# A gated decoder step: partial sums of the second projection added on chip, and the first chunk's loads moved from POOL's queue to ACT's

## The chip, the cores and the metric

The kernel runs on one core of one Trainium2 chip. The metric is device time in microseconds (us), from the start of the program to its end. A core has five engines with queues of their own: PE (TensorE, matrix products into the PSUM banks; PEld is its weight load), DVE (VectorE), ACT (ScalarE), POOL (GpSimd) and SP (SyncE, here only a DMA queue). SP, ACT and POOL issue DMAs, and an instruction that waits holds up everything behind it on its engine.

## The reference

One layer of a hybrid decoder over 1024 prompt tokens and 8 sample tokens (1032 columns in the kernel), D_MODEL 2048. Two branches, a retention and a diagonal state space model, are projected back to 2048 columns, gated, summed and projected once more:

```python
proj = h @ w_in
q, k, v, za, ub, zb, ga, gb = jnp.split(proj, splits, axis=-1)
ya, s_ret_new = retention(q, k, v, pos, s_ret)
ya = (ya * jax.nn.silu(za.astype(F32))).astype(x.dtype) @ w_pa
yb, s_re_new, s_im_new = s5(ub, ...)          # ends in a GLU: y * sigmoid(y @ w_glu + b_glu)
yb = (yb * jax.nn.silu(zb.astype(F32))).astype(x.dtype) @ w_pb
merged = jax.nn.sigmoid(ga) * ya + jax.nn.sigmoid(gb) * yb
out = merged @ w_out
return x + rmsnorm(out, g_post), s_ret_new, s_re_new, s_im_new
```

All is float32. The change concerns `merged` (the sum of the two gated projections) and the start of `merged @ w_out`.

## The kernel before, in words

Each float32 operand is split into two float32r halves, `hi` (a cast on ACT) and `lo` (the remainder, a subtraction on DVE), and a product is three matmuls: hi*hi, hi*lo, lo*hi. Every operand of PE thus costs one ACT cast and one DVE subtraction, for weights (`whi`, `wlo`) and tokens (`a`, function `split`).

The stages on PE in order: the input projection `w_in` in two halves of the contraction; the GLU (`w_glu`, lines 1475 and 1476); the gated projections `w_pa` (8 pairs of row tiles) and `w_pb` (8 pairs, p = 0 to 7); and `w_out`, first the last 392 tokens (`out_rows`, 16 outputs of 4 weight quarters each), then the first 640 (`out_tokens`).

The projections use a scheme of seven products per 2 x 2 block: for each pair of row tiles (2p, 2p+1) and two column halves of HT = 516 tokens, products n = 0 to 6, each 24 matmuls. `evac_p` takes a product out of PSUM, and the blocks "11", "22", "21", "12" are complete at n = 2, 4, 5, 6. The column half c is 1 for "22" and "12".

`gated` then multiplies a block by its gate `zz` (loaded on ACT's queue by `load_z` two products ahead). In `w_pa` the block is stored to `pap_d`. In `w_pb` POOL issues a DMA that adds the `pap_d` block onto the tile in place (`accum_op`), and LAG = 4 products later a second DMA that stores the merged tile to `mg_d`. Only the last pair's c = 1 blocks load `pap_d` to chip and add on DVE or POOL.

For `w_out` each of 16 merged row tiles m is split again. Tokens 640 to 1031 are needed first: tiles 0 to 11 are loaded back (`mg_load`, tile `mga`, on ACT's queue), tiles 12 to 15 are taken from the tiles still on chip (`last_t`; tiles 12 and 13 belong to pair 6, 14 and 15 to pair 7). Tokens 0 to 639 are loaded and split by `fill` while `out_rows` runs, through two slots of one large tile `z`.

The order on each engine is that of the code, with work put behind product g by `at(g, ...)` and run by `late_work(g)`; background generators in `bg` advance one `yield` per `slot()`, that is per product or per weight quarter. `left_over` runs what the last gate of `w_in` (sigmoids `u<-u`, `p<-p` on ACT after an accumulating DMA) still has due when the GLU starts.

Of the kernel before, what the change touches and what calls it, by code (L numbers as in the profile page):

```python
# [10 lines left out]
F32 = mybir.dt.float32  # L11
# [16 lines left out]
TA = 640  # L28
SW = TOK - TA
THIRDS = [(0, 384), (384, 768), (768, TOK), (TA, TOK)]  # L30
HT = TOK // 2
# [47 lines left out]
def emit(ctx, tc, I, O):  # L79
    nc = tc.nc  # L80
    V, A, P, T = nc.vector, nc.scalar, nc.gpsimd, nc.tensor

    def tt(out, a, b, op, eng=None):
        return (eng or V).tensor_tensor(out, a, b, op)  # L84

    def mul(out, a, b, eng=None):
        tt(out, a, b, ALU.mult, eng)

    def add(out, a, b, eng=None):
        return tt(out, a, b, ALU.add, eng)  # L90
# [34 lines left out]
    def dram(name, shape):  # L125
        return dr.tile(shape, F32, name=name)
# [18 lines left out]
    mg_d = dram("mg_d", [16, 128, TOK])  # L145
# [34 lines left out]
    def drain():  # L180
        while bg:
            slot()
# [617 lines left out]
    def popen(name, side, bufs):  # L800
        st = ExitStack()
        return st, st.enter_context(tc.tile_pool(name=name, bufs=bufs, side=side))
# [9 lines left out]
    NP = len(pairs)  # L812
    steps = [(kh, p) for kh in range(2) for p in range(NP)] + [(kh, p) for kh in ("pa", "pb") for p in range(8)]
# [83 lines left out]
    def two(t):  # L897
        return t.rearrange("p (j c) -> p j c", j=2)
# [9 lines left out]
    def at(g, f):  # L908
        due.setdefault(g, []).append(f)
# [324 lines left out]
    def late_work(g):  # L1234
        with ExitStack() as after:
            for ins in anchor.values():
                after.enter_context(tc.issue_after(ins))
            for f in due.pop(g, ()):
                f()
# [4 lines left out]
    for s in range(2 * NP):  # L1244
        kh, p = steps[s]
# [40 lines left out]
        for n in range(7):  # L1286
            g = 7 * s + n
# [28 lines left out]
    gstack.close()  # L1316

    def left_over():
        for n in range(2, 8):
            yield  # L1320
            for g in sorted(due):
                if g - 14 * NP <= n - (n > 4) - 2:
                    late_work(g)


# [5 lines left out]
    zz_tile = lambda: zzp.tile([128, HT], F32, name="zz")  # L1331
    opened = {}

    def fx_open():
        opened["fx"], opened["fxp"] = popen("fx", "left", 4)
# [145 lines left out]
    zq = {}  # L1481
    AT = {"11": (0, 0), "22": (1, 1), "21": (1, 0), "12": (0, 1)}
    last_t = {}

    def load_z(s, name):
        kind, p = steps[s]
        r, c = AT[name]
        zq[name] = zz_tile()
        A.dma_start(zq[name], (sga_d if kind == "pa" else sgb_d)[2 * p + r, :, HT * c:HT * c + HT])
        if s == len(steps) - 1 and c:  # L1490
            zq[name, "p"] = zz_tile()
            A.dma_start(zq[name, "p"], pap_d[2 * p + r, :, HT * c:HT * c + HT])

    def gated(g, name, t, ps=None):
        s = g // 7
        kind, p = steps[s]
        r, c = AT[name]
        m, cols = 2 * p + r, slice(HT * c, HT * c + HT)
        z = zq.pop(name)
        if ps is None:  # L1500
            mul(t, t, z)
        else:
            mul(two(t), ps, two(z))
        if kind == "pa":
            P.dma_start(pap_d[m, :, cols], t)
        elif (name, "p") in zq:
            add(t, t, zq.pop((name, "p")), P if name == "22" else V)
            last_t[m] = t
            P.dma_start(mg_d[m, :, HT:TA], t[:, 0:TA - HT])
        else:  # L1510
            P.dma_start(t, pap_d[m, :, cols], accum_op=ALU.add)
            at(g + LAG, lambda: P.dma_start(mg_d[m, :, cols], t))  # L1512
            if s == len(steps) - 2 and c:
                last_t[m] = t

    def evac_p(g, ps):
        n = g % 7
# [39 lines left out]
    SE = len(steps) - 1  # L1557
    mg_order = deque(range(2, 12))
    nxt = done_q = 0
    for s in range(S0, len(steps)):  # L1560
        kind, p = steps[s]
        if s == S0 + 1:
            opened["stg"].close()
            fx_open()
            bg.append(make_forms(yb_d, fb_d))
        if s == S0 + 6:
            drain()
            stg_open(8)
        if s == S0 + 9:
            opened["stg"].close()  # L1570
            mgstack, mgp = popen("mgp", "left", 6)
        for n in range(7):
            g = 7 * s + n
            if n == 1:
                fetch(s + 1)
            prep(g + 2)
            evac_p(g, product(g))
            if n in (0, 2, 3, 4):
                at(g, lambda s=s, n=n: load_z(s, {0: "11", 2: "22", 3: "21", 4: "12"}[n]))
            if s == S0 and n < 6:  # L1580
                for _ in range((2, 1, 1, 1, 2, 1)[n]):
                    at(g, lambda o=order_q[pa_q[0]]: unstage("pa", *o))
                    if pa_q[0] + 8 < 28:
                        at(g, lambda o=order_q[pa_q[0] + 8]: stage(opened["stgp"], "pa", *o))
                    pa_q[0] += 1
            q = g - 7 * (S0 + 6)
            if 0 <= q < 4:
                for _ in range(2):
                    at(g, lambda o=order_q[nxt]: stage(opened["stgp"], "pb", *o))
                    nxt += 1  # L1590
            if 3 <= q < 20:
                for i in range(1 if q < 7 else 2):
                    if done_q < 28:
                        at(g, lambda o=order_q[done_q]: unstage("pb", *o))
                        done_q += 1
                        if nxt < 28:
                            at(g, lambda o=order_q[nxt]: stage(opened["stgp"], "pb", *o))
                            nxt += 1
            if s == SE - 1 and n in (1, 2, 3):
                for m in (2 * n - 2, 2 * n - 1):  # L1600
                    at(g, lambda m=m: mg_load(m))
            if s == SE - 1 and n in (5, 6):
                at(g, lambda m=n - 5: mg_split(m))
            if s == SE and n < 6:
                for m in (2 + 2 * n, 3 + 2 * n):
                    at(g, lambda m=m: mg_split(m, last_t[m][:, TA - HT:HT] if m in last_t else None))
                for m in (6 + 2 * n, 7 + 2 * n) if n < 3 else ():
                    at(g, lambda m=m: mg_load(m))
            late_work(g)
            slot()  # L1610
    for m in (15, 14):
        mg_split(m, last_t[m][:, TA - HT:HT])
    for g in sorted(due):
        late_work(g)
    mgstack.close()
    zstack.close()
    estack.close()
# [18 lines left out]
    def out_rows():  # L1636
        t0, w, per = TA, TOK - TA, 5
        ssq = stl.tile([128, SW], F32, name="sp")[:, 0:w]
        rb = rstd[:, 0:w]
        zt, slots = {}, {}  # L1640
        slots[3] = free.pop()
        zt[3] = flat(slots[3])

        def fill():

            place = lambda m: zt[3][:, w + TA * (m % 2):w + TA * (m % 2) + TA]

            def ld(m):
                P.dma_start(place(m), mg_d[m, :, 0:TA])

            ld(0)
            ld(1)
            for m in range(KD):
                for _ in range(2):
                    yield
                split((mg[m][0][:, 0:TA], mg[m][1][:, 0:TA]), place(m))
                yield
                if m + 2 < KD:
                    ld(m + 2)

        bg.append(fill())

        def z_of(m):
            return zt[m // per][:, (m % per) * w:(m % per + 1) * w]

        def evac_out(m):
            def f(_, ps):
                if m < 15 and m % per == 0:
                    slots[m // per] = free.popleft()
                    zt[m // per] = flat(slots[m // per])  # L1670
                if m == 0:
                    A.activation(ssq, ps, AF.Square)
                else:
                    s = st_tile()[:, 0:w]
                    A.activation(s, ps, AF.Square)
                    add(ssq, ssq, s, P)
                A.activation(z_of(m), ps, AF.Copy, scale=gpost[:, m:m + 1])
            return f

        def finish():  # L1680
            yield
            yield
            yield from rms_bcast(ssq, rb, stl)
            for m in range(16):
                z = z_of(m)
                x = stl.tile([128, SW], F32, name="sz")[:, 0:w]
                nc.sync.dma_start(x, I["xT"][m, :, t0:TOK])
                yield
                mul(z, z, rb)
                add(z, z, x)  # L1690
                P.dma_start(O["yA"][m], z)
                if m % per == per - 1 or m == 15:
                    free.append(slots[m // per])
                yield

        for m in range(16):
            linear(I["w_out"], m, KD, lambda k: mg[k], evac_out(m), thirds=(3,))
        bg.append(finish())
# [182 lines left out]
```

## Time and profile before

| | us |
|---|---|
| median of 3 runs | 2634.81 (2631.14 to 2636.29) |
| the profiled execution, its own time | 2632.4 |
| its span in the trace | 2630.6 |
| PE busy | 2596.9 |
| the GLU's first and last matmul | 1822.1 and 1914.5 |
| last matmul of `w_pb` starts | 2237.5 |
| first matmul of `w_out` | 2246.1 |

The rows shown further down come from one profiled execution. A row of the timeline has the start, the duration, the engine, the line, the operation, the tile written and the tiles read, a count, and in brackets how long the engine stood idle before it and for what. A row of the waits reads "who <- for whom: total us, times, longest". A row of the windows has its bounds and length, then the busy time and instructions of each engine, the granted PE clock (1.00 is full), the busy share of the 16 DMA engines and GB/s. `u`, `p` and `st` are the tiles of a block, `pp` its partial sum after the change, `acc` and `mm` PSUM banks.

### The profile page before, as it was taken

The page shows a single profiled execution, that of the slowest core. Times are in us where ns is not written, and L with a number is a line of the kernel's source. Part 1 is how long each engine was busy: PE and PEld are TensorE (multiplying, and loading weights), DVE is VectorE, ACT ScalarE, POOL GpSimd, SP SyncE. Part 2 cuts the span into 40 slices and gives each one's busy share as a digit, 9 for nine tenths or more (in the row PEclk, how much of TensorE's full clock was granted, in tenths as well). Part 3 has the DMA queues.
Part 4 walks back from the last instruction along what each step waited for, and adds up shares of the span by engine and source line. Part 5 has one row for each costly group of instructions (what it writes and reads, how often), then busy time and mean ns, then how long its engine had stood idle before and what let it go on. Part 6 is the DMA issues. An engine that isn't in the chain of part 4 may idle for free. (4 is left out here: it accounts for less than half of the span.)

```text
span 2630.6 us, 51277 instructions
## 1 busy us (share of the span) xinstructions
PE 2596.9 (99%) x19652; PEld 2532.8 (96%) x19652; DVE 1840.2 (70%) x3852; ACT 956.6 (36%) x1679; POOL 716.5 (27%) x1173
## 2 busy tenths in 40 slices
PE   9999999999999999999999999999999999899998
PEld 8999999999999999999999999999999999798886
DVE  6655989889889867558876656666477866444555
ACT  6113233333323325443234544444332423343343
POOL 0103322222222222332244433333422322211011
PEclk9999999999999999999999999999999999899999
DMA  5896444444444457886689787869777788655666
GB/s 191 260 269 208 151 122 125 132 126 122 126 127 123 130 162 216 208 216 165 153 212 252 204 208 201 214 168 278 244 240 239 241 196 229 195 157 176 190 200 229
DMA packets 228789, 499.85 MB, mean 190 GB/s; under 512 B 32432, under 2 KB 54912, under 8 KB 228416
## 3 DMA queue, kind: packets, MB, share of 16 engines
q0 software_dynamic: 94704, 274.47, 38.2%
q1 hardware_dynamic: 103072, 179.57, 22.5%
q10 hardware_dynamic: 30768, 42.54, 5.4%
q8 instruction: 154, 2.52, 0.4%
q14 instruction: 91, 0.75, 0.1%
HBM read 340.57 MB, written 155.89 MB: 189 GB/s over the span
## 5 line engine op out<-in xcount | busy, mean ns | idle before, releaser
L892 PE MATMUL acc<-a,whi 128*128 128x258 f32 x9632 | 1562.3, 284 | 1.0 <-ACT whi L873 0.6
L892 PEld LDWEIGHTS acc<-a,whi 128*128 128x128 f32 x9632 | 1326.6, 190 | 5.4 <-issue 2.4
L892 PE MATMUL acc<-a,wlo 128*128 128x258 f32 x4816 | 969.1, 282 | 0.0
L892 PEld LDWEIGHTS acc<-a,wlo 128*128 128x128 f32 x4816 | 744.7, 189 | 0.0
L84 DVE TENSOR_TENSOR wlo<-wraw,whi 128x512 fp32r<-128x512 f32 x482 | 331.2, 687 | 242.9 <-ACT whi L202 139.9
L873 ACT CAST whi<-wraw 128x512 fp32r<-128x512 f32 x344 | 213.8, 622 | 618.5 <-PE acc L892 508.0
L873 ACT CAST whi<-wr 128x512 fp32r<-128x512 f32 x258 | 160.3, 621 | 515.6 <-PE acc L892 442.0
L209 PE MATMUL mm<-a,whi 128*128 128x384 f32 (+2 forms) x704 | 235.0, 335 | 17.6 <-ACT whi L202 9.4
L210 PE MATMUL mm<-a,whi 128*128 128x384 f32 (+2 forms) x704 | 234.4, 333 | 0.2 <-DVE a L363 0.2
L211 PE MATMUL mm<-a,wlo 128*128 128x384 f32 (+2 forms) x704 | 233.4, 332 | 0.1
L84 DVE TENSOR_TENSOR wlo<-wr,whi 128x512 fp32r<-128x512 f32 x273 | 187.2, 686 | 50.4 <-ACT whi L873 29.8
L1779 PE MATMUL mm<-whi,a 128*128 128x512 f32 x512 | 171.1, 395 | 0.0
L202 ACT CAST whi<-wraw 128x512 fp32r<-128x512 f32 x138 | 85.5, 621 | 205.0 <-PE mm L210 95.3
L209 PEld LDWEIGHTS mm<-a,whi 128*128 128x128 f32 x704 | 133.8, 190 | 18.7 <-ACT whi L202 9.9
L211 PEld LDWEIGHTS mm<-a,wlo 128*128 128x128 f32 x704 | 134.5, 191 | 1.7 <-DVE wlo L84 1.6
L210 PEld LDWEIGHTS mm<-a,whi 128*128 128x128 f32 x704 | 134.1, 190 | 1.0 <-DVE a L363 0.9
L84 DVE TENSOR_TENSOR wraw<-wr 128x512 f32<-128x512 f32 x172 | 118.2, 687 | 7.0 <-DMA wr<-in_w_pa 4.7
L1779 PEld LDWEIGHTS mm<-whi,a 128*128 128x128 f32 x512 | 96.2, 188 | 22.8
L84 DVE TENSOR_TENSOR p<-acc,p 128x516 f32<-128x516 f32 x86 | 59.6, 693 | 81.7 <-PE acc L892 81.5
L84 DVE TENSOR_TENSOR u<-acc,u 128x516 f32<-128x516 f32 x86 | 59.7, 694 | 63.1 <-PE acc L892 61.8
L84 DVE TENSOR_TENSOR u<-acc,p 128x516 f32<-128x516 f32 x86 | 59.6, 693 | 62.5 <-PE acc L892 62.1
L1779 PE MATMUL mm<-wlo,a 128*128 128x512 f32 x256 | 101.3, 396 | 0.0
(368 smaller groups left out, 3423.4 us busy)
## 6 DMA issues: line engine op xcount, KB each, us to landing
wr<-in_w_in SPq DMA_DIRECT2D x280, 256.0 KB
pt_d<-u POOLq DMA_DIRECT2D x70, 258.0 KB, 3.3
u<-pt_d POOLq DMA_DIRECT2D x70, 258.0 KB, 5.2
wraw<-in_w_outB SPq DMA_DIRECT2D x66, 256.0 KB
stg<-fm_d POOLq DMA_DIRECT2D x44, 258.0 KB, 4.4
wx<-in_w_outB SPq DMA_DIRECT2D x43, 256.0 KB
wraw<-in_w_out SPq DMA_DIRECT2D x39, 256.0 KB
pt_d<-st POOLq DMA_DIRECT2D x35, 258.0 KB, 3.1
```

The costliest lines, as they stand in the source:

```text
L84: return (eng or V).tensor_tensor(out, a, b, op)
L202: anchor["a"] = A.copy(hi, raw).ins
L209: T.matmul(ps, wh[:, i, :], xh[:, t0:t1], start=first, stop=False)
L210: T.matmul(ps, wh[:, i, :], xl[:, t0:t1], start=False, stop=False)
L211: anchor["p"] = T.matmul(ps, wl[:, i, :], xh[:, t0:t1], start=False, stop=last).ins
L873: anchor["a"] = A.copy(hi, f).ins
L892: anchor["p"] = T.matmul(ps[:, j, 0:258], a[:, i, :], b[:, 258 * j:258 * j + 258], start=first and i == 0 and a is wh and b is xh, stop=n ...
L1779: anchor["p"] = T.matmul(ps[c], a, b, start=k == 0 and a is xh and b is wh, stop=k == KD - 1 and a is xl).ins
```

## The change

- `load_z` loads the partial sum `pap_d` into a new pool `pp` of four tiles for every block from pair 2 on, on ACT's queue, right behind the block's gate.
- `gated` adds it on DVE (on POOL for three blocks of the last pair) and stores the merged tile at once, all its columns. Pairs 0 and 1 keep the accumulating DMA. `mga` has five tiles in place of six, and its first loads are spread over the pair before the last.
- `fill` issues its loads on ACT's queue, a slot later than before, and gives the first one six slots before its split in place of two.
- `left_over` runs the last gate's three sigmoid steps at slots 4, 6 and 9. On ACT the last of them then stands behind the first three GLU evacuations (L1423) and not ahead of them, and three casts of the forms for `w_pa` (`a<-fx`), not two, stand ahead of the first.

```diff
     def left_over():
-        for n in range(2, 8):
+        for n in range(12):
             yield
             for g in sorted(due):
-                if g - 14 * NP <= n - (n > 4) - 2:
+                if n >= {1: 4, 2: 6, 3: 9}[g - 14 * NP]:
                     late_work(g)
...
-        if s == len(steps) - 1 and c:
-            zq[name, "p"] = zz_tile()
+        if kind == "pb" and p > 1:
+            zq[name, "p"] = ppp.tile([128, HT], F32, name="pp")
             A.dma_start(zq[name, "p"], pap_d[2 * p + r, :, HT * c:HT * c + HT])
...
         elif (name, "p") in zq:
-            add(t, t, zq.pop((name, "p")), P if name == "22" else V)
-            last_t[m] = t
-            P.dma_start(mg_d[m, :, HT:TA], t[:, 0:TA - HT])
+            add(t, t, zq.pop((name, "p")), P if p == 7 and name != "12" else V)
+            if c and p > 5:
+                last_t[m] = t
+            P.dma_start(mg_d[m, :, cols], t)
         else:
             P.dma_start(t, pap_d[m, :, cols], accum_op=ALU.add)
             at(g + LAG, lambda: P.dma_start(mg_d[m, :, cols], t))
-            if s == len(steps) - 2 and c:
-                last_t[m] = t
...
-            mgstack, mgp = popen("mgp", "left", 6)
+            mgstack, mgp = popen("mgp", "left", 5)
+            ppstack, ppp = popen("pp", "left", 4)
...
-            if s == SE - 1 and n in (1, 2, 3):
-                for m in (2 * n - 2, 2 * n - 1):
+            if s == SE - 1 and n in (1, 2, 5, 6):
+                for m in (2 * n - 2, 2 * n - 1) if n < 3 else (n - 1,):
                     at(g, lambda m=m: mg_load(m))
...
             def ld(m):
-                P.dma_start(place(m), mg_d[m, :, 0:TA])
-
+                A.dma_start(place(m), mg_d[m, :, 0:TA])
+
+            yield
             ld(0)
             ld(1)
             for m in range(KD):
-                for _ in range(2):
+                for _ in range(2 if m else 6):
                     yield
```

How the built program moves, at three places. POOL, from the last pair's first block on, before (`z` is the large tile of the output stage, `sp` and `st` at the end are sums of squares there):

```order
L1511 DMA st<-pap_d 128x516
L1512 DMA mg_d<-st 128x516
L84 TENSOR_TENSOR u_27954<-u_27954,zz 128x516
L1509 DMA mg_d<-u_27954 128x124
L1511 DMA p_27822<-pap_d 128x516
L1512 DMA mg_d<-p_27822 128x516
L1509 DMA mg_d<-u_27867 128x124
L1632 DMA z_28106<-in_g_post_row 128x2048
L1649 DMA z_28110<-mg_d 128x640 x5
```

The same stretch of POOL after the change:

```order
L84 TENSOR_TENSOR st<-st,pp 128x516
L1510 DMA mg_d<-st 128x516
L84 TENSOR_TENSOR u_28001<-u_28001,pp 128x516
L1510 DMA mg_d<-u_28001 128x516
L84 TENSOR_TENSOR p_27868<-p_27868,pp 128x516
L1510 DMA mg_d<-p_27868 128x516
L1510 DMA mg_d<-u_27915 128x516
L1633 DMA z_28154<-in_g_post_row 128x2048
L84 TENSOR_TENSOR sp<-sp,st 128x392 x15
```

The accumulating DMAs (L1511) and the loads of the 640-token chunk (L1649) have left this queue.

DVE around the last PSUM evacuation, which is `u_27867<-acc` before (`a<-u` are the second halves of the splits of tiles 12 to 15, `wlo` those of weights):

```order
L84 TENSOR_TENSOR u_27954<-u_27954,zz 128x516
L84 TENSOR_TENSOR a_28037<-u_27602,a_28037 128x392
L84 TENSOR_TENSOR wlo<-wraw,whi 128x512
L84 TENSOR_TENSOR p_27822<-acc,p_27822 128x516
L84 TENSOR_TENSOR a_28040<-u_27675,a_28040 128x392
L84 TENSOR_TENSOR p_27822<-p_27822,zz 128x516
L84 TENSOR_TENSOR wlo<-wraw,whi 128x512
L84 TENSOR_TENSOR u_27867<-acc,u_27867 128x516
```

After the change it is `u_27915<-acc`:

```order
L84 TENSOR_TENSOR p_27868<-acc,p_27868 128x516
L84 TENSOR_TENSOR a_28086<-u_27642,a_28086 128x392
L84 TENSOR_TENSOR p_27868<-p_27868,zz 128x516
L84 TENSOR_TENSOR a_28089<-u_27716,a_28089 128x392
L84 TENSOR_TENSOR wlo<-wraw,whi 128x512
L84 TENSOR_TENSOR u_27915<-acc,u_27915 128x516
L84 TENSOR_TENSOR a_28120<-u_28001,a_28120 128x392
L84 TENSOR_TENSOR u_27915<-u_27915,zz 128x516
L84 TENSOR_TENSOR wlo<-wraw,whi 128x512
L84 TENSOR_TENSOR u_27915<-u_27915,pp 128x516
```

The two splits of pair 6's tiles now stand behind the evacuation of n = 5, and a sum `u<-u,pp` follows the last gate.

ACT from the last weight casts of the gated stage into `w_out`, before (`whi` are casts of weight quarters, `a<-z` of the 640-token chunk):

```order
L256 CAST a_28075<-u_27867 128x392
L202 CAST whi<-wx_28105 128x512
L202 CAST whi<-wraw 128x512 x2
L1672 ACTIVATE sp<-mm 128x392
L1677 ACTIVATE z_28192<-mm,gpost 128x392
L202 CAST whi<-wraw 128x512
L256 CAST a_27751<-z_28110 128x640
```

And after:

```order
L256 CAST a_28123<-u_27915 128x392
L202 CAST whi<-wx_28153 128x512
L1650 DMA z_28158<-mg_d 128x640 x2
L202 CAST whi<-wraw 128x512 x2
L1674 ACTIVATE sp<-mm 128x392
L1679 ACTIVATE z_28238<-mm,gpost 128x392
L202 CAST whi<-wraw 128x512
L202 CAST whi<-wx_28152 128x512
L256 CAST a_27795<-z_28158 128x640
```

The first two loads stand between the fifth and the sixth weight cast of `w_out`, and in the built program they wait for the stores of the six last merged tiles but the `st` ones, since `z` lies over those buffers. In the built program each DMA of SP or ACT also waits for the DMA that used its completion semaphore last, of eight that the two queues take in turn: a pair had eight such DMAs (four weights, four gates) and now has twelve.

More of the change, by code (lines that the diff above doesn't have):

```diff
@@ L1614, in emit @@
         late_work(g)
+    ppstack.close()
     mgstack.close()
```

## The prediction

> **What bounds the kernel now.** I read the page's busy shares and clock row first, then the list of waits of TensorE (PE), then PE's own rows around each wait, and from there the engine that each wait names.
>
> ```profile
> PE 2596.9 (99%) x19652; PEld 2532.8 (96%) x19652; DVE 1840.2 (70%) x3852; ACT 956.6 (36%) x1679; POOL 716.5 (27%) x1173
> PEclk9999999999999999999999999999999999899999
> ...
> PE mm L209 <- ACT whi L202: 9.4, 2, 5.2
> PE mm L209 <- DVE u L84: 8.2, 1, 8.2
> PE acc L209 <- ACT p L1423: 1.3, 1, 1.3
> ...
> PE acc L209 <- ACT u L1423: 0.4, 1, 0.4
> ```
>
> PE is the bound: 99% busy, and the clock row has one slice under full. So a change pays only where PE stands still or runs slowly. Of the waits (total, times, longest), 5.2 us of the first line is the load at the kernel's start. What stays is 8.2 and 4.2 us, both at the seam between the last gated product and the output projection, and 1.3 + 0.4 us early in the GLU. The windows of the seam:
>
> ```profile
> core 0: us, PE busy (x) PEld busy (x) DVE busy (x) ACT busy (x) POOL busy (x), PEclk, DMA share, GB/s
> ...
> 2206.00:2238.00 32.00, 31.91 (x264) 31.52 (x263) 21.62 (x36) 12.08 (x23) 8.96 (x12) 1.00 0.93 255
> 2238.00:2246.10 8.10, 0.00 (x0) 0.01 (x1) 4.19 (x8) 2.06 (x4) 2.07 (x3) 0.68 0.71 164
> 2246.10:2251.20 5.10, 5.08 (x16) 5.10 (x17) 1.36 (x3) 0.83 (x2) 2.43 (x4) 0.50 0.67 223
> 2251.20:2265.90 14.70, 14.69 (x82) 14.35 (x80) 4.82 (x8) 4.09 (x8) 3.62 (x6) 1.00 0.75 218
> 2265.90:2270.10 4.20, 0.04 (x1) 0.04 (x1) 1.40 (x2) 2.06 (x4) 0.54 (x1) 0.78 0.37 127
> 2270.10:2275.10 5.00, 5.00 (x15) 4.56 (x16) 2.99 (x6) 3.17 (x6) 2.06 (x3) 0.50 0.80 238
> ```
>
> After each hole the granted clock is 0.50 for about 5 us: 16 and 15 matmuls, where the full-clock window does 82 in 14.70, that is 0.179 us each. Each hole therefore costs its idle time and a slow restart. Why the first hole lasts:
>
> ```profile
> 2226.43 0.70 DVE L84 TENSOR_TENSOR st<-acc,zz 128x516 f32<-128x516 f32 x1
> 2242.13 0.93 POOL L1511 DMA_DIRECT2D st<-pap_d  x1
> POOL mg_d L1512 <- DMA u<-pap_d: 47.1, 14, 6.8
> ...
> 2241.36 0.52 ACT L256 CAST a<-u 128x392 fp32r<-128x392 f32 x1 [6.71 <-DMA u<-pap_d]
> 2241.91 0.57 DVE L84 TENSOR_TENSOR a<-u,a 128x392 fp32r<-128x392 f32 x1 [6.04 <-ACT a L256]
> 2245.28 0.69 DVE L84 TENSOR_TENSOR u<-acc,u 128x516 f32<-128x516 f32 x1
> 2246.12 0.67 PE L209 MATMUL mm<-a,whi 128*128 128x392 f32 x1 [8.21 <-DVE u L84]
> ```
>
> POOL issues the accumulating DMA and behind it, in order, the store that must wait for it. It is 15.0 us late by the last pair (2226.43 + 0.70 to 2242.13). So the sum of row tile 12 arrives late, ACT's cast of it waits 6.71 us, DVE's half of that split waits for ACT, and the last PSUM evacuation (u<-acc,u) stands behind it on DVE; PE can't have the banks before. The second hole hangs on the same queue: POOL gets to the first loads of the 640-token chunk only at 2260.92, ACT blocks on one, and the weight casts queue behind.
>
> ```profile
> 2260.92 1.16 POOL L1649 DMA_DIRECT2D z<-mg_d  x2
> 2266.82 0.72 ACT L256 CAST a<-z 128x640 fp32r<-128x640 f32 x1 [5.81 <-DMA z<-mg_d]
> 2270.06 0.69 PE L209 MATMUL mm<-a,whi 128*128 128x392 f32 x1 [4.17 <-ACT whi L202]
> ```
>
> **The change, part by part.**
>
> *First hole.* From pair 2 on, 22 accumulating DMAs leave POOL (of 30; two sums of the last pair were made on chip already), and no store there waits for a DMA any more. The casts of tiles 12 and 13 need only a DVE add of the pair before. In the new order DVE meets, after evacuation n=5 (PE ends at 2246.12 - 8.21 = 2237.91; at 264 matmuls in 31.91 us its product of 24 takes 2.9, so n=5 is ready at 2235.0): a cast's remainder, the gate, a second remainder and one weight remainder, then the last evacuation: with n=5 itself five operations ahead of it of 0.56 to 0.70 us, which brings the start of the last one to about 2238.0, 0.1 us after PE's end. From the start of that evacuation to PE's start the rows above show 0.84 us (2245.28 to 2246.12). So 0.95 us of the 8.21 remain: gain 7.3. The upper end is 7.4 (no lateness). For the lower end there is one row of doubt, the loads of tiles 10 and 11 that stand ahead:
>
> ```profile
> ACT a L256 <- DMA mga<-mg_d: 2.7, 2, 2.0
> ```
>
> If that wait, now hidden, came a second time, 3.7 us would remain and the gain be 4.5. I take 7.3: these loads are issued at the same product as before, with POOL's backlog gone.
>
> *Clock after it.* 5.10 - 16 x 0.179 = 2.2 us. A pause of 0.95 us is nearer to the one of 1.34 us in the GLU than to the 4.17:
>
> ```profile
> 1833.40:1834.90 1.50, 0.16 (x3) 0.01 (x1) 1.02 (x2) 1.45 (x3) 1.07 (x2) 1.00 0.99 402
> 1834.90:1840.00 5.10, 4.67 (x25) 4.35 (x26) 5.07 (x10) 3.14 (x6) 2.05 (x4) 1.00 0.75 240
> ```
>
> There the clock stayed at 1.00. So the 2.2 us go (0 if the pause stays long).
>
> *Second hole.* The loads move to ACT, issued about one weight quarter into the first output row, and the first split waits six quarters in place of two. But the first load has to wait for the last store of a merged tile, whose buffer lies under it. That store follows, on DVE, the last evacuation, a remainder, the gate, a weight remainder and the new add (0.6 us a step from 2238.0): issued at 2241.4.
>
> ```profile
> DMA to landing us min/median/max: 1.9/3.6/7.2
> L1551 ACTq DMA_DIRECT2D mga<-mg_d x12: 326/378/499, 2200.8 to 2226.9; - x12
> ```
>
> The first row is of all DMAs on the merged tensor. With the median the store lands at 2245.0 and ACT, having issued both loads (2 x 0.4), casts the sixth quarter by 2246.4. PE, started at 2238.9, needs it four quarters of 12 x 0.179 = 2.15 us later, at 2247.5. Behind the waiting issue on ACT stand just these weight casts. With the maximum of 7.2 it would be 2.5 us late. So of 4.17 remain 0 to 2.5; I take the median, 0. The split itself comes about 13 us after the loads; the old one, 6 us after, had to wait 5.81. Clock after it: 5.00 - 15 x 0.179 = 2.3 us, which goes too.
>
> *Added work.* 22 more loads on ACT and 20 more adds on DVE, 2 on POOL.
>
> ```profile
> L84 DVE TENSOR_TENSOR u<-u,zz x15: 687/692/696, 2092.4 to 2235.2; 128x516 f32<-128x516 f32 x15
> ACT whi L873 <- PE acc L892: 81.2, 40, 2.3
> DMA to landing us min/median/max: 2.3/5.8/8.5
> ```
>
> Four adds of 0.69 us a pair (20.2 us) are 2.8 us on an engine that is busy 21.62 of 32: covered. Of that cover little is left beside the last twelve splits, and there the adds of the last pair but one go to POOL. ACT's casts wait for PE about 2 us each, so 0.4 us of issue costs nothing. Each partial sum is issued three products (8.6 us) ahead of its add; the last row, landings of the same tensor now, has a maximum of 8.5. So zero, with up to 1 us against it. The full stores in place of 124 columns: no one waits but the loads already counted.
>
> *GLU.* The late sigmoids of the last gate are spread out.
>
> ```profile
> 1832.70 0.64 ACT L972 ACTIVATE u<-u 128x516 f32<-128x516 f32 x1 [2.83 <-DMA u<-pt_d]
> 1834.27 0.57 ACT L1423 ACTIVATE p<-acc,bglu 128x384 f32<-128x384 f32 x1
> ```
>
> The last of them, waiting 2.83 us for its DMA, no longer stands ahead of the first GLU evacuation at 1834.27, but one more cast of the forms does. I step these through with DVE's 0.69 us a piece and get the evacuation 0.7 to 1.1 us earlier. Of 1.34 + 0.43 us I take 1.0; the bounds are -0.5 (the forms' second tile lands late; a store now stands behind a load on POOL) and 1.8.
>
> **Sum:** 7.3 + 2.2 + 4.2 + 2.3 + 1.0 = 17.0 us off the profiled execution's 2632.4 (span 2630.6) gives 2615.4. The median shown is 2.4 above that execution, so 2617.8.
>
> [...]
>
> **Rivals.**
> 1. *The holes shrink but stay long enough for the slow clock.* Tile loads 2.74 us later and the last store at its maximum: 3.7 us remain in the first hole and 2.5 in the second, each followed by its slow stretch. Gain 17.0 - 2.7 - 2.2 - 2.5 - 2.3 = 7.3, time 2627.5. For it: DMA share 0.93 just ahead of the seam, and a margin of 1.1 us at the second. Against: less for POOL to do, and the GLU's 1.34.
> 2. *Slower.* The place is ACT's queue at the fourth gate of a pair and the first of the next: in the new order their loads share completion semaphores with that pair's four weight loads and can't issue before those have landed. A weight cast runs two products (5.8 us) ahead, less 0.62 for the cast and 0.69 for the remainder: 4.4 us to spare. If ACT waited the 8.5 us of the slowest landing at both gates of five pairs, PE would lose 10 x (8.5 - 4.4) = 41 us: 2659. It outweighs the gain from a wait of 6.1 us at each (10 x 1.7 = 17). Against: the weight loads are issued 8.6 us before ACT gets there.
> 3. *Nothing.* The transfers themselves are the limit: 0.93 of the DMA engines, the same 258 KB a tile. The tiles come as late as now, both holes stay, and only the GLU's 1.0 is won: 2633.8. Against: POOL waited for one DMA at a time, and the share falls to 0.37 in the second hole.
>
> **How the numbers follow.** Forecast 0.72, first rival 0.16, second 0.05, third 0.07. A measurement here tells about 0.2% (5.3 us) from no change. Faster: all of the forecast and three quarters of the first rival, 0.84; same: the rest of it and the third, 0.11; slower 0.05. The forecast's own range is 2613 (bounds 7.4, 4.2 and 1.8, from the lowest run, 2631.1) to 2622 (the last store at its maximum, from the highest run: 2636.3 - 14.5). The range reaches to the first rival with the runs' scatter (2627.5 and 1.5 for the highest run over the median): 2612.5 to 2629, leaving out the second and third.
>
> **What would show it.** PE's waits at the seam: the one on DVE under 1.5 us and none on ACT's weight cast; granted clock 1.00 through the seam; POOL's waits on accumulating DMAs left to the first two pairs; ACT's cast of the first 640-token tile without a wait. Wrong it would be with ACT waiting at its own partial-sum issues and PE for whi in the gated pairs (rival 2), with DVE's adds waiting for pp, or with a clock of 0.50 again after the seam (rival 1).

## The result and the profile after

The changed kernel takes 2618.3 us (median of 4 runs, 2617.2 to 2620.2) against 2633.8 us for the kernel before (4 runs, 2631.1 to 2636.3): a ratio of 0.9942, 95% interval 0.9925 to 0.9959, that is 15.5 us faster. The forecast was 2617.8. The profiled execution took 2618.5 us (span 2616.7), 13.9 us less than the one of before.

The page's busy and clock rows, and then the list of PE's waits (who waits for whom: total, times, longest):

```profile
PE 2592.8 (99%) x19652; PEld 2531.2 (97%) x19652; DVE 1855.9 (71%) x3872; ACT 955.0 (36%) x1679; POOL 688.8 (26%) x1137
PEclk9999999999999999999999999999999999999999
...
PE mm L209 <- ACT whi L202: 5.0, 1, 5.0
PE mm L209 <- DVE u L84: 2.8, 1, 2.8
PE acc L209 <- ACT p L1423: 1.4, 1, 1.4
```

The 5.0 us are the kernel's start as before. The 4.2 us at the seam are gone, the 8.2 us are 2.8, the GLU has one wait in place of two. The same stretch in windows (PE, PEld, DVE, ACT, POOL, granted clock, DMA share, GB/s): the last products of `w_pb`, the hole, the five and then fifteen microseconds behind it.

```profile
2206.00:2236.80 30.80, 30.80 (x257) 30.63 (x256) 26.82 (x43) 13.13 (x25) 6.31 (x8) 1.00 0.78 252
2236.80:2239.70 2.90, 0.07 (x2) 0.06 (x1) 2.90 (x4) 1.04 (x2) 2.08 (x2) 1.00 0.03 11
2239.70:2244.70 5.00, 5.00 (x20) 5.00 (x21) 3.85 (x7) 1.04 (x2) 0.54 (x1) 0.66 0.75 252
2244.70:2259.70 15.00, 15.00 (x85) 15.00 (x84) 5.52 (x9) 6.40 (x12) 0.61 (x2) 1.00 0.73 258
```

In the hole the DMA engines do almost nothing (0.03) and DVE works all 2.90 us: the transfers are no longer what is late, DVE is. Behind it the clock is 0.66 for five microseconds, not 0.50, and the second hole does not come. POOL's waits on accumulating DMAs, 29 times and 114.5 us before, are 8 times and 34.2 us, all in the first two pairs:

```profile
POOL mg_d L1513 <- DMA u<-pap_d: 16.4, 4, 5.4
...
POOL mg_d L1513 <- DMA st<-pap_d: 11.1, 2, 6.3
...
POOL mg_d L1513 <- DMA p<-pap_d: 6.7, 2, 5.1
```

What DVE does in the hole, from the timeline (POOL, DVE and PE rows, put in order of time engine by engine):

```profile
2233.11 1.54 POOL L84 TENSOR_TENSOR u<-u,pp 128x516 f32<-128x516 f32 x1 [4.57 <-DMA zz<-sgb_d]
2236.85 1.52 POOL L84 TENSOR_TENSOR p<-p,pp 128x516 f32<-128x516 f32 x1 [1.35 <-DVE p L84]
...
2229.45 1.04 DVE L84 TENSOR_TENSOR a<-mga,a 128x392 fp32r<-128x392 f32 x2
2231.73 0.69 DVE L84 TENSOR_TENSOR wlo<-wraw,whi 128x512 fp32r<-128x512 f32 x1
2232.93 2.14 DVE L84 TENSOR_TENSOR a<-mga,a 128x392 fp32r<-128x392 f32 x2
2235.00 0.68 DVE L84 TENSOR_TENSOR p<-acc,p 128x516 f32<-128x516 f32 x1
2237.16 1.76 DVE L84 TENSOR_TENSOR wlo<-wraw,whi 128x512 fp32r<-128x512 f32 x1
2238.84 0.68 DVE L84 TENSOR_TENSOR u<-acc,u 128x516 f32<-128x516 f32 x1
...
2239.67 0.41 PE L209 MATMUL mm<-a,whi 128*128 128x392 f32 x1 [2.83 <-DVE u L84]
```

Two subtractions of a token remainder take 1.04 us at 2229.45 and 2.14 us at 2232.93; a weight remainder takes 0.69 us at 2231.73 and 1.76 us at 2237.16. Each long one lies where POOL adds (2233.11 to 2234.65, 2236.85 to 2238.37), and each is 1.1 us too long: it ends about half a microsecond after POOL's add (2235.07 after 2234.65, 2238.92 after 2238.37), as if the last piece of it had waited for that. A third long pair, 2.14 us at 2225.97 beside POOL's add of 2226.19 to 2227.68, was made up before the seam. The last evacuation (`u<-acc,u`) stands behind both and starts at 2238.84, 2.0 us after PE's end at 2236.84.

The second hole's chain, with the last store of before in the first row, and a row of ACT's waits ahead of the weight casts of the gated pairs (2080 to 2275 us):

```profile
2256.30 0.55 POOL L1509 DMA_DIRECT2D mg_d<-u  x1
...
2242.11 0.54 POOL L1510 DMA_DIRECT2D mg_d<-u  x1 [2.89 <-DVE u L84]
...
2246.11 0.81 ACTq L1650 DMA_DIRECT2D z<-mg_d  x2
2254.75 0.72 ACT L256 CAST a<-z 128x640 fp32r<-128x640 f32 x1
...
ACT whi L873 <- DMA zz<-sgb_d: 24.9, 11, 2.3
```

The last store is issued 14.2 us earlier than before (2242.11 against 2256.30, where the loads followed at 2260.92), the loads go out at 2246.11, and the cast finds its tile landed. The last row names a DMA on ACT's queue, and such waits are more than before (24.9 us, 11 times, against 15.8 us, 7 times), but it is a change of name only: all waits ahead of these casts together are 101.0 us, 49 times, against 100.0 us, 49 times, and no single one is longer than 2.3 us in either. ACT has that time to spare in both kernels.

### The profile page after: what moved, and what is told of

Read it like the earlier page. It is cut to its first block, busy times and chain, and to the rows that moved or that the text cites. A ratio compares the mean times of both kernels' runs of the same rounds, so it can differ in the third digit from the quotient of the medians.

```text
span 2616.7 us, 51319 instructions
## 1 busy us (share of the span) xinstructions
PE 2592.8 (99%) x19652; PEld 2531.2 (97%) x19652; DVE 1855.9 (71%) x3872; ACT 955.0 (36%) x1679; POOL 688.8 (26%) x1137
## 5 line engine op out<-in xcount | busy, mean ns | idle before, releaser
L84 DVE TENSOR_TENSOR wlo<-wx,whi 128x512 fp32r<-128x512 f32 x76 | 52.5, 692 | 71.0 <-ACT whi L202 70.4
```

## The experiments

Ten executions can be laid side by side in two stretches: from the first GLU matmul that waited to the end of `w_pb` on PE (T0, the start of the matmul behind the hole less its wait), and from T0 to the end of PE's last matmul. The last column is the median of the runs. The runs of the experiments were made in two groups on two chips: the kernel before took 2633.25 us (15 runs, 2628.0 to 2637.9) beside the changed kernel once more, the adds on DVE, the late sum's first run and the new loads alone, and 2636.05 us (9 runs) beside the other four, so medians are compared within a group, and across the groups only the ratios to the kernel before.

| kernel | GLU to T0 | waits at the seam | clock, some 5 us behind the first | T0 to PE's last | runs, us |
|---|---|---|---|---|---|
| before | 403.01 | 8.21 + 4.17 | 0.50 | 380.81 | 2633.8 |
| after | 402.06 | 2.83 | 0.66 | 367.84 | 2618.3 |
| after, once more | 402.07 | 2.82 | 1.00 | 366.27 | 2617.65 |
| all the last pair's adds on DVE | 402.07 | 1.38 + 2.07 | 1.00, then 0.52 | 368.72 | 2619.9 |
| last sum late, first weights early | 402.07 | 1.38 | 1.00 | 365.16 | 2617.3 |
| the same once more | 402.08 | 1.37 | 1.00 | 365.13 | 2616.3 |
| before, with the new loads alone | 402.77 | 7.30 + 1.20 | 0.53 | 374.66 | 2625.7 |
| after, with the old loads | 402.08 | 2.83 | 0.66 | 367.79 | 2617.4 |
| sums on chip in two pairs only | 403.80 | 2.39 | 1.00 | 365.94 | 2618.5 |
| after, with the old GLU spacing | 402.77 | 2.82 | 1.00 | 366.26 | 2619.3 |

From PE's last matmul to the end of the span each has 10.3 to 10.6 or 11.9 to 12.1 us, and the difference lies behind DVE's last operation. The three short ones are the new loads alone, the old loads and the sums in two pairs, each profiled once; why they are shorter stays open.

**The changed kernel once more**, as the standard for the runs beside it, without an edit.

> The changed kernel again, on the chip of the others of this group, as their yardstick: 2618 us, 0.994 of the kernel before; PE's wait on DVE at the seam 2.8 us, with a stretch at half clock behind it.

2617.65 us (5 runs, 2616.8 to 2619.1), ratio 0.9946 [0.9932, 0.996]. The hole is the same, but the clock is not. The first two rows are this run's, a PE row and the window of the five microseconds behind the hole:

```profile
2240.39 0.41 PE L209 MATMUL mm<-a,whi 128*128 128x392 f32 x1 [2.82 <-DVE u L84]
...
2240.39:2245.39 5.00, 5.00 (x28) 5.00 (x29) 3.91 (x7) 1.60 (x3) 0.54 (x1) 1.00 0.74 243
```

And the same window of the first execution:

```profile
2239.67:2244.67 5.00, 5.00 (x19) 5.00 (x20) 3.85 (x7) 1.04 (x2) 0.54 (x1) 0.66 0.73 248
```

28 matmuls against 19 in the same five microseconds: a pause of 2.82 or 2.83 us costs one execution 1.5 us of slow clock and another nothing. 0.66 over five microseconds is 3.4 us at half rate; the windows between 2240.70 and 2243.20 us of the first execution show 0.50. What decides between the two no run shows.

**All adds of the last pair on DVE**, so that POOL has none at the seam.

```diff
-            add(t, t, zq.pop((name, "p")), P if p == 7 and name != "12" else V)
+            add(t, t, zq.pop((name, "p")), V)
```

> The three adds of the last pair that the changed kernel gives to POOL are done by DVE. Theory (a POOL add holds DVE up while it runs: three DVE stretches of 1.1 us too long): the stretches are gone, each add costs DVE 0.69, the last evacuation starts at most 0.6 us after PE's end, PE's wait on it is 1.0 to 1.5 us in place of 2.8, though the first weight remainder of the output stage now stands behind it and may cost PE another 0.5 to 1 us; 1 to 3 us faster than the changed kernel. Rival (DVE merely has too much to do there): three adds more lengthen PE's wait to 4 us or more, and the kernel is 1 to 3 us slower.

2619.9 us (2619.6 to 2620.3), ratio 0.9954 [0.9942, 0.9967]: 2.3 us more than the changed kernel beside it (2616.8 to 2619.1). The DVE row that was 2.14 us long, PE's two waits and the window behind them:

```profile
2234.19 1.04 DVE L84 TENSOR_TENSOR a<-mga,a 128x392 fp32r<-128x392 f32 x2
...
2238.75 0.42 PE L209 MATMUL mm<-a,whi 128*128 128x392 f32 x1 [1.38 <-DVE u L84]
2240.68 0.68 DVE L84 TENSOR_TENSOR wlo<-wraw,whi 128x512 fp32r<-128x512 f32 x1
2241.41 0.44 PE L211 MATMUL mm<-a,wlo 128*128 128x392 f32 x1 [2.07 <-DVE wlo L84]
...
2243.00:2246.50 3.50, 3.50 (x13) 3.50 (x12) 1.33 (x3) 0.62 (x1) 0.23 (x1) 0.52 0.88 279
```

Without POOL's adds the long operations are short again and the hole is 1.38 us: that POOL's adds hold DVE up is thereby shown. But the first weight remainder of `w_out` now stands behind the last evacuation and its successors on DVE, so PE stops again two matmuls on, and half clock follows the two pauses (0.52). A wait was exchanged for another. The time is the one that the rival gave, 1 to 3 us slower, though not for its reason: PE's wait on the evacuation became shorter, not 4 us or more.

**The last sum put behind the last evacuation, and the first weights fetched earlier**, both aimed at that second wait.

```diff
-            add(t, t, zq.pop((name, "p")), P if p == 7 and name != "12" else V)
+            pp = zq.pop((name, "p"))
+            def summed():
+                add(t, t, pp, V)
+                P.dma_start(mg_d[m, :, cols], t)
...
-            P.dma_start(mg_d[m, :, cols], t)
+            if p == 7 and name == "21":
+                at(g + 1, summed)
+            else:
+                summed()
...
+            if s == SE and n == 5:
+                todo.extend((I["w_out"], m, kq) for m in range(16) for kq in range(4))
+                fetch_w()
```

> As the run with all adds on DVE, but the last pair's 21 block is added behind the last evacuation, and the first output weight is split one product earlier, so that neither stands between PE's end and the evacuation. Theory: PE's wait on DVE is 1.0 us, the granted clock stays 1.00 through the seam, and the time is 3.4 us under the changed kernel (1.9 of the hole, 1.5 of the half clock). Rival (DVE has too much to do): the time is that of the changed kernel or more.

2617.3 us (2615.6 to 2618.2), ratio 0.9943 [0.993, 0.9955]. Its hole, the evacuation's place and the window:

```profile
2240.59 0.41 PE L209 MATMUL mm<-a,whi 128*128 128x392 f32 x1 [1.38 <-DVE u L84]
...
2240.70:2245.00 4.30, 4.26 (x23) 3.92 (x24) 4.30 (x8) 1.39 (x3) 1.08 (x2) 1.00 0.39 123
```

One wait of 1.38 us, full clock, and the shortest stretch from T0 to PE's last matmul of all, 365.2 us. Of the 3.4 us that were expected the median shows 0.4. The 1.38 us are above the 1.0 expected, the changed kernel loses the 1.5 us of slow clock in some of its executions only, and the profiled execution lost 2.0 us in an earlier stage, where PE waited for ACT and ACT for a load. So it went once more:

> The same kernel as in the run with the late sum put behind the last eviction and the first weights fetched earlier, once more, since its one profile had 2.0 us of wait elsewhere (TensorE waited for ACT, which waited for a load of an earlier stage) that says nothing of this seam. Theory A: the seam is worth 2.7 us (376 to 378 us from the end of the gated projection to the end, where the changed kernel has 379.9), and the median is 2615 to 2616.5. Rival B: what the seam gives is lost behind it in every run, and the median is 2617.2 to 2618.

2616.3 us (2615.0 to 2616.8), ratio 0.9926 [0.9913, 0.9938], and 365.13 us behind T0. The two profiles agree that the seam is 1.1 us shorter than the changed kernel's at full clock and 2.7 us shorter than with the slow stretch. Over the whole kernel that is 0.04 to 0.1%; its two ratios (0.9943 and 0.9926) and the changed kernel's two (0.9942 and 0.9946) don't separate, their intervals overlap, and the changed kernel was not run beside the second of them, so it is shown in the trace and not in the time.

**The kernel before with the new loads alone** (the change's third part without the sums).

```diff
-                P.dma_start(place(m), mg_d[m, :, 0:TA])
+                A.dma_start(place(m), mg_d[m, :, 0:TA])
+            yield
...
-                for _ in range(2):
+                for _ in range(2 if m else 6):
```

> The kernel before with the new fill alone: the 640-token loads on ACT's queue, later and with more slots ahead of the split; the sums are still made by accumulating DMAs on POOL. Theory (POOL's 15 us of lateness is the cause of both holes): the first hole stays 8.2 us; the first load on ACT still has to wait for the last merged store, issued by the late POOL at 2256 and landed at 2260, so ACT blocks there and PE loses 0 to 4 us in a second hole; 2630 to 2634, at most 4 us under the kernel before. Rival (the second hole comes from the queue and the short lead alone): it goes with its slow clock, 6.4 us faster, 2627.

2625.7 us (11 runs, 2624.8 to 2631.1), ratio 0.9979 [0.9969, 0.9989]: about half the gain by the medians. Of the 7.6 us between the profiles 6.15 lie between T0 and PE's last matmul, 0.9 of them in the first hole, which was shorter with nothing edited ahead of it, and 1.4 behind PE's last matmul. PE's two waits at the seam, with ACT's issue and cast between them:

```profile
2245.10 0.66 PE L209 MATMUL mm<-a,whi 128*128 128x392 f32 x1 [7.30 <-DVE u L84]
...
2257.85 0.81 ACTq L1649 DMA_DIRECT2D z<-mg_d  x2
2258.76 1.14 ACT L202 CAST whi<-wraw 128x512 fp32r<-128x512 f32 x2 [6.45 <-PE mm L211]
2259.43 0.45 PE L209 MATMUL mm<-a,whi 128*128 128x392 f32 x1 [1.20 <-ACT whi L202]
```

I had expected POOL's backlog to keep the second hole, since the last store is as late as ever. It is, and ACT's issue at 2257.85 does hold the weight casts behind it (the 6.45 us stand against PE, but the issue ahead went out 0.9 us before the casts); yet PE loses 1.20 us there, not 4.17, and no slow clock follows (1.00 over the five microseconds from 2259.43), because the casts wait for the store alone and no longer for the load and the split as well. My theory fell in this execution and in the median. But the profile is of the fastest of the eleven, and four runs took 2630.2 to 2631.1 us, inside the theory's range; what they lost no trace shows.

**The changed kernel with the old loads** (POOL's queue, no slot ahead, two slots to the first cast): the sums without the third part.

```diff
-                A.dma_start(place(m), mg_d[m, :, 0:TA])
+                P.dma_start(place(m), mg_d[m, :, 0:TA])
-            yield
...
-                for _ in range(2 if m else 6):
+                for _ in range(2):
```

> The on-chip sums stay; the loads of the merged tokens go back to POOL's queue and to their old places (no slot ahead of the first, two slots before the first cast), so this is the change without its third part. Theory A (the second hole came from POOL's backlog of accumulating transfers alone, which put the last store at 2256.3 us and the loads behind it at 2260.9): the last store is now issued at about 2242.8 and the loads at about 2247.4, right behind the norm's row; by the 5.9 us that the first load took in the kernel before it lands at about 2253.3, ACT casts two tiles and then the weight that TensorE needs at about 2256.8, so the second wait is 0 to 0.5 us and the time is 2617.7 to 2618.5. Rival B (the place and the lead are needed as well, as the run with the new loads alone suggested, where they took away nearly 3 of 4.2 us): the second wait on ACT's weight cast comes back with 1.5 to 4 us and part of its half clock, and the time is 2620 to 2624.

2617.4 us (2615.2 to 2621.2), ratio 0.9931 [0.9919, 0.9944], like the changed kernel. Its loads on POOL, the casts and the one wait of PE:

```profile
2244.10 0.41 PE L209 MATMUL mm<-a,whi 128*128 128x392 f32 x1 [2.83 <-DVE u L84]
...
2250.75 1.07 POOL L1650 DMA_DIRECT2D z<-mg_d  x2
2257.01 0.72 ACT L256 CAST a<-z 128x640 fp32r<-128x640 f32 x1
2258.03 0.73 ACT L256 CAST a<-z 128x640 fp32r<-128x640 f32 x1 [0.30 <-DMA z<-mg_d]
```

The first cast finds its tile there, the second waits 0.30 us, PE not at all: theory A. Once the sums have emptied POOL's queue, the move of the loads is worth nothing (367.79 against 367.84 us behind T0). Either part takes the second hole away, or nearly (for the loads alone that holds for the profiled execution); the gains don't add.

**Sums on chip in the last two pairs only.**

```diff
-        if kind == "pb" and p > 1:
+        if kind == "pb" and p > 5:
```

> The changed kernel, but partial sums are loaded and added on chip only in the last two of the eight pairs; pairs three to six keep the accumulating transfer. Theory A (only transfers in the last pairs can reach the seam; POOL works off the earlier ones within the pairs behind them): POOL's waits on accumulating transfers come back to about 12 of 28 tiles, some 60 us, but the seam is as in the changed kernel, with 2.8 us on DVE's last store, and the time is 2617.7 within 1 us. Rival B (POOL's backlog adds up from pair to pair, so that the last pairs' adds and stores still come late): the first wait is 4 us or more and the time is 2620 or above. Rival C (the sums of the middle pairs cost DVE and ACT something that TensorE feels in the changed kernel): 2616.5 or below.

2618.5 us (2616.9 to 2619.2), ratio 0.9934 [0.9922, 0.9947]. POOL's longest row of waits, its stores of pair 6 and PE's wait at the seam:

```profile
POOL mg_d L1513 <- DMA u<-pap_d: 38.5, 12, 6.7
...
2221.41 0.57 POOL L1513 DMA_DIRECT2D mg_d<-u  x1 [1.03 <-DMA u<-pap_d]
2221.97 0.54 POOL L1510 DMA_DIRECT2D mg_d<-st  x1
2223.56 0.54 POOL L1510 DMA_DIRECT2D mg_d<-u  x1
...
2240.96 0.42 PE L209 MATMUL mm<-a,whi 128*128 128x392 f32 x1 [2.39 <-DVE u L84]
```

A is right on the seam and on the time: 2.39 us at full clock, no longer than in the changed kernel. B's forecast, 4 us or more there, failed, but its mechanism is in the trace: the backlog does add up over pairs. POOL waits 23 times and 92.7 us on accumulating DMAs, not the 12 times and 60 us of A, and gets to the four stores of pair 6 only at 2221.97 and after, when it is done with the accumulated tiles of pair 5. ACT's copies of L1519, the last of them at 2223.3, wait for the store of a tile `p` (5.3 us in two waits), and PE 1.5 us for a copy, which it doesn't in the changed kernel:

```profile
PE acc L892 <- ACT p L1519: 1.5, 1, 1.5
```

That is the 1.7 us more before T0 in the table. C is out: the run is no faster, and the middle pairs' sums cost PE no wait.

**The changed kernel with the old GLU spacing.**

```diff
-        for n in range(12):
+        for n in range(2, 8):
...
-                if n >= {1: 4, 2: 6, 3: 9}[g - 14 * NP]:
+                if g - 14 * NP <= n - (n > 4) - 2:
```

> The changed kernel with the old spacing of the late groups of work ahead of the gated pairs (the function that spreads them over slots 2 to 7 instead of 12). Theory A: the wait of TensorE at the first gated unit goes from 1.40 us back to the 1.34 and 0.43 us of the kernel before, and the time is 0.5 to 1.0 us more than the changed kernel's 2617.65, that is 2618.2 to 2618.7; the waits in the profile tell it better than the time. Rival B: TensorE is ahead of ACT there in any case and gives the time back within the same stage, so the waits change and the end doesn't: 2617.65 within 0.4.

2619.3 us, but 2616.9 to 2623.6 over five runs, so the time tells nothing. The waits come back as A said:

```profile
1834.07 0.44 PE L209 MATMUL acc<-a,whi 128*128 128x384 f32 x1 [1.46 <-ACT p L1423]
1836.87 0.44 PE L209 MATMUL acc<-a,whi 128*128 128x384 f32 x1 [0.43 <-ACT u L1423]
```

From the first of them to T0 it has 402.77 us where the six executions with the new spacing and sums from the third pair have 402.06 to 402.08: the spacing is worth 0.7 us there. The first wait lies ahead of that stretch and tells nothing: it is 1.10 to 1.79 us in the executions with the new spacing and 1.30 to 1.46 in those with the old. The rows of the changed kernel show what stands ahead of it now:

```profile
1833.62 0.62 ACT L256 CAST a<-fx 128x516 fp32r<-128x516 f32 x1 [1.14 <-DVE fx L84]
1834.15 0.57 ACT L1423 ACTIVATE p<-acc,bglu 128x384 f32<-128x384 f32 x1
1834.78 0.45 PE L209 MATMUL acc<-a,whi 128*128 128x384 f32 x1 [1.40 <-ACT p L1423]
```

The late sigmoid is no longer ahead of the first evacuation, but a cast of the forms is, and it waits 1.14 us for DVE.

## Why the prediction was right, term by term

The profiled spans differ by 13.9 us: 0.12 up to the GLU's row, 0.95 from there to T0, 12.97 from T0 to PE's last matmul, and 0.14 the other way in what follows it. The sum had 17.0.

- *First hole*: 7.3 forecast, 5.4 measured (8.21 to 2.83). The mechanism was right: POOL's queue is empty, and the casts of the tiles of pair 6 don't wait for a transfer. The step that was mis-sized is the one that put five operations of 0.56 to 0.70 us ahead of the last evacuation and its start 0.1 us after PE's end. It started 2.0 us after. The evacuation of n=5, the first of the five, began 1.1 us late (2235.00, with its product ready 2.9 us ahead of PE's end, at 2233.9), behind the long token remainder, and the weight remainder among the five took 1.1 us longer, both beside POOL's adds. The prediction moved those adds to POOL and counted them as free there. The bound of 3.7 us that it gave for lateness held, though for another reason than the late `mga` loads that it was worked out from: ACT's wait for one of them, at 2230.03, is 0.67 us and was made up by 2234.
- *Clock behind it*: 2.2 forecast. A pause of 2.83 us lies between the 1.34 (full clock) and the 4.17 (half) that the prediction had, and it goes either way: 1.5 us stayed in one execution, nothing in another. The forecast compared it with the wrong end because it had the pause at 0.95.
- *Second hole and its clock*: 4.2 and 2.3, both gone as forecast, PE's 85 matmuls in 15.00 us at 1.00. The prediction gave the move to ACT's queue a part in it; the run with the old loads shows that the sums do it alone. Its estimate of the last store, issued at 2241.4 and landed at 2245.0, was near: it went out at 2242.11, and the loads that wait for it at 2246.11.
- *Added work*: nothing forecast from loads and DVE's adds, and nothing found ahead of T0: with the old spacing the GLU to T0 takes 402.77 us both with the sums and without them (the new loads alone). ACT's waits ahead of its casts are the same in sum and at most 2.3 us, as before, below the 4.4 us to spare from which the second rival would have begun to cost. The adds did cost something where the prediction also put nothing, on POOL at the seam; that is counted in the first hole.
- *GLU*: 1.0 forecast, 0.7 by the experiment, but not in the way forecast. The first evacuation was to come 0.7 to 1.1 us earlier. It comes 12.24 us after the GLU's first matmul (1821.91 to 1834.15), against 12.18 before (1822.09 to 1834.27), and PE's wait for it is 1.40 us against 1.34. What went is the second wait, 0.43 us, and some of what follows it.

Together: the first hole fell short by 1.9 us and its clock by 1.5 in the profiled execution; the rest came out within 0.3. That the median still hit to 0.5 us is luck. The sum put the profiled execution at 2615.4 us and it took 2618.5, 3.1 more; but the forecast then added 2.4 us because the median of before lay that much above its profile, and after the change the median lies 0.2 below its profile. By the gain itself, 15.5 us in the medians and 13.9 in the profiles against 17.0, the forecast was too high. (The lower end of the range, 2612.5, is also half a microsecond below the 2613 that the prediction works out.)

Of the signs that it named, those of the second hole and of POOL came (POOL's waits left to the first two pairs, the cast without a wait, and none of PE on ACT's weight cast), and the two of the first hole failed: the wait on DVE is 2.83 us, not under 1.5, and the clock at the seam was 1.00 in the second profile but 0.66 in the first. So the first rival (long holes) is half true at the first hole: 2.83 us is nearer to its 3.7 than to 0.95, and the slow clock followed in two of four such executions, though late loads were not the cause. At the second hole, and in the time, it is out. The second didn't happen; the third (the transfers as the limit) is refuted by the DMA share of 0.03 in the hole and 0.78 ahead of it.

What the sum missed is what POOL's adds do to DVE. The trace gives the price: DVE's subtractions take 1.1 us more beside a POOL add of 1.5 us, and end only after it (2235.07 after 2234.65, 2238.92 after 2238.37). How the one holds the other up, no run shows.

## What to carry to other kernels

An engine that has time to spare is not free to use: around the moved operation, read the durations of the operations on the critical engine, not only their order (here 0.69 us became 1.76). When two parts of a change cure the same wait, run each alone before crediting both. And take a second execution before the price of a pause is put down: the same 2.8 us cost 1.5 us of slow clock or nothing.

## What the runs showed of the hardware

- A POOL add of two 128x516 float32 tiles (1.5 us) lengthens DVE's 0.69 us subtraction beside it to 1.76 us, and a pair of 1.04 us to 2.14. Without the POOL add they are short again (0.69 and 1.04 us with all the last pair's adds on DVE). POOL's own operation of that size (a product) takes 1.30 us in the kernel before, at 2249.03, where DVE stands idle.
- A pause of PE of 2.8 us was followed by half clock (0.66 over five microseconds, some 3.4 us at half rate) in two of four executions with the same instructions at the seam and by full clock (1.00) in the other two; 2.39 us left it at 1.00 in one profile and 1.4 us in two, and 1.38 and 2.07 us with 0.6 us of work between them were followed by 0.52.
- From PE's last matmul to the end, the same work took 10.3 to 10.6 us in three of ten executions and 11.9 to 12.1 in seven. The difference lies behind DVE's last operation; what decides it stays open.
